# A decoder trunk on one core: five of the eleven block pairs of the last product by seven products of quarters

## The chip, the core and the metric

The kernel runs on one core of a Trainium2 chip. A core has a matrix engine (TensorE, PE in the profile, with its weight loads shown as PEld), a vector engine (VectorE, DVE), a scalar engine (ScalarE, ACT), a general engine (GpSimd, POOL) and a queue that issues most transfers (SyncE, SP). The metric is the device time of one launch in microseconds. Before the change it is 992.31 us, the median of three runs (992.31 to 992.92).

## The reference

The input is x, 256 tokens of 1024 features, in float32. Two layers follow each other, and each has the same three parts: a half-weighted SwiGLU feed-forward step, attention (dilated windows in the first layer, block-sparse in the second, whose keys and values are computed once from the stream after the first layer), and another half-weighted SwiGLU step. A final RMSNorm ends it. The change is in the last feed-forward step and what follows it:

```python
def swiglu(h, w_gate, w_up, w_down):
    return (jax.nn.silu(h @ w_gate) * (h @ w_up)) @ w_down

h = h + 0.5 * swiglu(rmsnorm(h, ffn2_norm[1]), ffn2_w_gate[1], ffn2_w_up[1], ffn2_w_down[1])
return rmsnorm(h, final_norm)
```

Here w_gate and w_up are 1024 x 2816 and w_down is 2816 x 1024. Everything is float32. The kernel reaches that by splitting each factor into a high part, rounded to a type that the matrix engine takes in one pass, and a low part, the remainder; a product is then three matmuls: high by high, high by low, low by high.

## The kernel before

The stream is kept with the features on the partitions (hT, eight tiles of 128 features by 256 tokens). A feed-forward step has two stages.

The gate and up stage is `ffn_blocks`. The 2816 hidden features are 22 blocks of 128, taken in eleven pairs. For a pair, the weights are loaded by SyncE into a raw tile (four of those exist), ScalarE writes their high parts (wh, line 153) and VectorE their low parts (wl, line 154); eight wh and eight wl buffers of 1024 columns exist. TensorE computes gate (f_g) and up (f_u) for a block (lines 193 and 196), and `close` makes the activation of the block: ScalarE and VectorE join the sums (lines 336, 337), VectorE scales (line 352), ScalarE applies the silu (line 353), GpSimd scales the up part (line 355), VectorE multiplies (line 356), and `parts_of` splits the product into a high part on ScalarE (line 94) and a low part on VectorE (line 90). The result is one act tile per block, high and low.

The last down product is `down_last`. Here the tokens are on the partitions of the output: two halves t of 128 tokens, and each output row has two halves c of 512 features. For each of the 22 blocks k, the act tile of k (128 x 128 for a token half) is the stationary factor and row block k of w_down the moving one. Two blocks come in one load of 1 MB (raw_f_d); each is split as above (wh_f_d, wl_f_d). Blocks 0 to 17 go to all accumulators in turn. The last four blocks are held back, so that the accumulators end one after another: for each, VectorE adds half of it to h (line 431), and `finish_part` and `finish` make the norm and send the rows out. The accumulator of the second token half and the second feature half is kept as two of 256 columns, so that the very last step is short. The order in which each engine takes its instructions comes from a scheduler that goes by the program's order, by what is ready in its own model, and by free buffers; on the chip each engine then runs its queue in that order and waits by semaphores.

The trace leaves digits out of names: dn_f21_d is dn_f_d there.

Of the kernel before, what the change touches and what calls it, by code (L numbers as in the profile page):

```python
# [25 lines left out]
NG = H // HG  # L26
ROT = 16
HALF = ROT // 2
LEAD = 4
EPS = 1e-6  # L30
SCALE = DH ** -0.5
# [31 lines left out]
def trunk(ctx: ExitStack, tc: tile.TileContext, a: dict, out: bass.AP):  # L63
    nc = tc.nc
    PS = bass.MemoryType.PSUM
    const = ctx.enter_context(tc.tile_pool(name="const", bufs=1))
    rawp = ctx.enter_context(tc.tile_pool(name="rawp", bufs=4))
    wp = ctx.enter_context(tc.tile_pool(name="wp", bufs=8))
    xp = ctx.enter_context(tc.tile_pool(name="xp", bufs=1))
# [30 lines left out]
    def trt(name):  # L100
        return trp.tile([P, 512], F32, tag="tr", name=name)
# [74 lines left out]
    def rows(w, k0, k, c0, n):  # L176
        return w[k0 * P:(k0 + k) * P, c0:c0 + n].rearrange("(k p) n -> p k n", p=P)

    def product(accs, xh, xl, ws, first, last):

        for ac, (wh, wl) in zip(accs, ws):
            nc.tensor.matmul(ac, xh, wh, start=first, stop=False)  # L182
        for ac, (wh, wl) in zip(accs, ws):
            nc.tensor.matmul(ac, xh, wl, start=False, stop=False)  # L184
        for ac, (wh, wl) in zip(accs, ws):
            nc.tensor.matmul(ac, xl, wh, start=False, stop=last)  # L186
# [94 lines left out]
    class Pieces:  # L281
# [6 lines left out]
        def load(self, u):  # L288
            while len(self.raws) <= min(u, len(self.specs) - 1):
                name, k, n, srcs = self.specs[len(self.raws)]  # L290
                raw = rawp.tile([P, k, n], F32, tag="raw", name=f"raw_{name}")
                for dst, src in srcs:
                    nc.sync.dma_start(raw if dst is None else raw[:, :, dst], src)
                self.raws.append(raw)

        def split(self, i):

            end = 2 * len(self.specs)
            while len(self.parts) <= min(i, end - 1):
# [37 lines left out]
        nc.vector.tensor_add(s, ac[:, :S], s)  # L337
        return s

    def ffn_blocks(name, wg, wu, norm, first=None, beside=()):  # L340

        blocks = []

        def both(f, pair):
            acs = [acc(f"{name}_{n}{f}") for n in "gu"]
            cols = slice(f % 2 * P, (f % 2 + 1) * P)
            products_t(acs, [[(wh[:, cols], wl[:, cols]) for wh, wl in w] for w in pair], norm.x, True, True)
            return acs

        def close(f, gate, up):  # L350
            g = joined(gate, f"{name}_g{f}")
            nc.vector.tensor_mul(g, g, norm.row)  # L352
            nc.scalar.activation(g, g, AF.Silu)  # L353
            u = joined(up, f"{name}_u{f}")
            nc.gpsimd.tensor_tensor(u, u, norm.row, op=ALU.mult)  # L355
            nc.vector.tensor_mul(g, g, u)  # L356
            x = atile([P, 2, S], F32R, name=f"act_{name}_{f}")
            parts_of(x[:, 0], x[:, 1], g)
            blocks.append(x)

        done = []

        def close_all():
            if done and norm.row is None:
                norm.spread()
            for args in done:
                close(*args)
            done.clear()

        for f in range(0, KF, 2):  # L370
            if f == 0 and first is not None:
                ws = opening(wg, wu, first)
            else:
                ws = zip(*[unit(f"{name}_{n}{f}", KD, S, [(None, rows(w, 0, KD, f * P, S))])
                           for n, w in (("g", wg), ("u", wu))])
            if f == 0:
                acs = [[(trt if i and n == "u" else acc)(f"{name}_{n}{i}") for n in "gu"] for i in range(2)]
                for k, pair in enumerate(ws):
                    for i in range(2):
                        for ac, (wh, wl) in zip(acs[i], pair):  # L380
# [24 lines left out]
        down_t(name, wd, blocks, after)  # L405


    def down_last(name, w, nk, blocks, h, weight, part, after, tail=4):


        segs = [[(0, 0, 512), (1, 0, 512)], [(0, 0, 512), (1, 0, 256), (1, 256, 256)]]
        accs = [[acc(f"dn_{name}_{t}_{c}_{o}")[:, :n] for c, o, n in segs[t]] for t in range(NT)]
        held = []

        def cols(t, ws):
            return [tuple(w[:, c * 512 + o:c * 512 + o + n] for w in ws) for c, o, n in segs[t]]

        for u in range(nk // 2):
            for i, ws in enumerate(unit(f"{name}_{u}", 2, D, [(None, rows(w, 2 * u, 2, 0, D))])):
                k = 2 * u + i  # L420
                if k < nk - tail:
                    for t in range(NT):
                        product(accs[t], *blocks[t][k], cols(t, ws), k == 0, False)
                else:
                    held.append((k, ws))
        for t in range(NT):
            for i, (c, o, n) in enumerate(segs[t]):
                for k, ws in held:
                    product(accs[t][i:i + 1], *blocks[t][k], cols(t, ws)[i:i + 1], False, k == nk - 1)
                hc = h[t][c][:, o:o + n]  # L430
                nc.vector.scalar_tensor_tensor(hc, accs[t][i], weight, hc, op0=ALU.mult, op1=ALU.add)
                part(t, slice(c * 512 + o, c * 512 + o + n))
            after(t)

    def out_t(name, pieces, base, blocks, norm, tail=3):
# [226 lines left out]
    w = a["a_w_qkv"][0]  # L662
# [12 lines left out]
        return [(n3, xkv, [wk]), (n5, xq, [wq]), (n3, xkv, [wv])]  # L675

    mixer("b", segs_b, a["b_w_o"][0], masks[:, 1, :], n6)
    blocks = ffn_blocks("f21", a["ffn2_w_gate"][1], a["ffn2_w_up"][1], n6)

    h = [[xp.tile([P, 512], F32, tag=f"kx{2 * t + c}", name=f"h_{t}_{c}") for c in range(2)] for t in range(NT)]  # L680
    for t in range(NT):
# [22 lines left out]
    def finish(t):  # L704
# [8 lines left out]
        for c in range(2):  # L713
            (nc.scalar, nc.sync)[c].dma_start(out[0, t * P:(t + 1) * P, c * 512:(c + 1) * 512], outs[t][c])

    down_last("f21_d", a["ffn2_w_down"][1], KF,
              [[tuple(x[:, i, t * P:(t + 1) * P] for i in range(2)) for x in blocks] for t in range(NT)],
              h, 0.5, finish_part, finish)


_INS = ["ffn1_w_gate", "ffn1_w_up", "ffn1_w_down", "ffn2_w_gate", "ffn2_w_up", "ffn2_w_down",
# [23 lines left out]
```

## Time and profile before

| what | value |
|---|---|
| median of three runs | 992.31 us |
| the profiled execution, its own time | 992.2 us |
| its span, first to last instruction | 990.4 us |
| granted TensorE clock, mean | 0.999 |
| TensorE busy | 979.6 us (99%) |
| VectorE busy | 731.3 us (74%) |
| ScalarE busy | 589.2 us (59%) |
| GpSimd busy | 163.6 us (17%) |
| the last down product, first to last matmul | 922.8 to 984.3 us |

A row of a timeline gives the start, the duration, the engine, the line, the operation, what is written and read, and in brackets the idle time ahead of it with what ended it. Matmuls overlap, so their durations are longer than the time from one start to the next; starts are what to compare. A row of a stage table gives the stretch, its length, then busy time and count of TensorE, its weight loads, VectorE, ScalarE and GpSimd, then the granted clock, the share of the transfer engines and their GB/s.

### The profile page before, as it was taken

The numbers are of one execution on the slowest core, as the hardware profiler recorded it, in microseconds if no ns is written. First come the engines' busy times: TensorE is split into PE (matmuls) and PEld (weight loads), VectorE is DVE, ScalarE is ACT, GpSimd is POOL, SyncE is SP. The second block draws the span as 40 slices with busy tenths as digits, with TensorE's granted clock in tenths as the row PEclk, the third lists the DMA queues.
The fourth block names the chain that finished last, engine by engine and source line by source line (L and its number), as shares of the span: only waits on it lengthen the run. The fifth ranks groups of instructions, "written<-read, shape, count | busy, mean of one in ns | idle before, by whom it ended". The sixth has DMA issues, their size and how long they took to land. (4 is left out here: it accounts for less than half of the span.)

```text
span 990.4 us, 15816 instructions
## 1 busy us (share of the span) xinstructions
PE 979.6 (99%) x5949; PEld 866.1 (87%) x5949; DVE 731.3 (74%) x1284; ACT 589.2 (59%) x1084; POOL 163.6 (17%) x195
## 2 busy tenths in 40 slices
PE   9999999999999999999999999999999999999997
PEld 6888888888899888888888888888889998888886
DVE  7988866667787887776678878666687778888542
ACT  6756554467776656645455666544676766655531
POOL 3211101122202211111021111111222032111000
PEclk9999999999999999999999999999999999999999
DMA  9876565654444466556646664666534445565511
GB/s 306 259 251 200 167 225 172 209 179 144 139 129 146 153 211 187 188 192 197 200 146 203 190 202 149 216 197 203 170 129 128 129 146 176 190 182 201 211 45 43
DMA packets 158398, 176.08 MB, mean 178 GB/s; under 512 B 3568, under 2 KB 152304, under 8 KB 158320
## 3 DMA queue, kind: packets, MB, share of 16 engines
q1 hardware_dynamic: 157888, 174.50, 54.8%
q8 instruction: 47, 0.77, 0.3%
q10 hardware_dynamic: 432, 0.55, 0.2%
q14 instruction: 31, 0.25, 0.1%
HBM read 173.99 MB, written 1.05 MB: 177 GB/s over the span
## 5 line engine op out<-in xcount | busy, mean ns | idle before, releaser
L193 PE MATMUL f_g<-x_n,wh_f_g 128*128 128x512 f32 x688 | 180.0, 394 | 0.0
L193 PE MATMUL f_u<-x_n,wh_f_u 128*128 128x512 f32 x688 | 177.6, 390 | 0.0
L193 PEld LDWEIGHTS f_u<-x_n,wh_f_u 128*128 128x128 f32 x688 | 129.0, 188 | 27.2
L193 PEld LDWEIGHTS f_g<-x_n,wh_f_g 128*128 128x128 f32 x688 | 124.1, 189 | 22.7
L355 POOL TENSOR_TENSOR j_f_u<-j_f_u,r_n 128x256 f32<-128x256 f32 x88 | 77.3, 880 | 378.1 <-DVE j_f_u L337 361.1
L193 PE MATMUL dn_f<-act_f,wh_f 128*128 128x512 f32 x528 | 126.5, 391 | 0.0
L154 DVE TENSOR_TENSOR wl_f_u<-raw_f_u,wh_f_u 128x1024 fp32r<-128x1024 f32 x86 | 120.8, 1406 | 1.8 <-ACT wh_f_u L153 1.7
L154 DVE TENSOR_TENSOR wl_f_g<-raw_f_g,wh_f_g 128x1024 fp32r<-128x1024 f32 x86 | 102.9, 1225 | 17.7 <-PE f_g L196 12.0
L193 PEld LDWEIGHTS dn_f<-act_f,wh_f 128*128 128x128 f32 x528 | 96.8, 188 | 18.6
L154 DVE TENSOR_TENSOR wl_f<-raw_f,wh_f 128x1024 fp32r<-128x1024 f32 x72 | 81.8, 1153 | 36.0 <-ACT wh_f L153 26.8
L196 PE MATMUL f_u<-x_n,wl_f_u 128*128 128x256 f32 x688 | 103.3, 283 | 0.0
L196 PE MATMUL f_g<-x_n,wl_f_g 128*128 128x256 f32 x688 | 102.7, 282 | 0.0
L196 PEld LDWEIGHTS f_g<-x_n,wl_f_g 128*128 128x128 f32 x688 | 96.4, 190 | 6.3
L153 ACT ACTIVATE wh_f_g<-raw_f_g 128x1024 fp32r<-128x1024 f32 x86 | 89.4, 1049 | 13.4 <-issue 6.0
L153 ACT ACTIVATE wh_f<-raw_f 128x1024 fp32r<-128x1024 f32 x72 | 67.3, 979 | 49.5 <-PE dn_f L193 30.3
L153 ACT ACTIVATE wh_f_u<-raw_f_u 128x1024 fp32r<-128x1024 f32 x86 | 86.6, 1047 | 15.7 <-PE f_g L193 10.9
L196 PEld LDWEIGHTS f_u<-x_n,wl_f_u 128*128 128x128 f32 x688 | 91.7, 192 | 0.1
L230 POOL TENSOR_TENSOR ss_n<-ss_n,sq_n 128x256 f32<-128x256 f32 x42 | 41.7, 992 | 246.5 <-ACT sq_n L229 245.6
L94 ACT ACTIVATE act_f<-j_f_g 128x256 fp32r<-128x256 f32 x88 | 36.5, 417 | 73.2 <-DVE j_f_g L356 73.1
L353 ACT ACTIVATE j_f_g<-j_f_g 128x256 f32<-128x256 f32 x88 | 36.7, 417 | 62.5 <-DVE j_f_g L352 62.1
L196 PEld LDWEIGHTS dn_f<-act_f,wl_f 128*128 128x128 f32 x528 | 68.1, 191 | 2.8
L196 PE MATMUL dn_f<-act_f,wl_f 128*128 128x256 f32 x528 | 69.0, 283 | 0.0
(213 smaller groups left out, 1798.1 us busy)
## 6 DMA issues: line engine op xcount, KB each, us to landing
raw_f_g<-in_ffn_w_gate_dram SPq DMA_DIRECT2D x43, 1024.0 KB, 5.4
raw_f_u<-in_ffn_w_up_dram SPq DMA_DIRECT2D x43, 1024.0 KB, 5.4
raw_f<-in_ffn_w_down_dram SPq DMA_DIRECT2D x24, 1024.0 KB, 5.0
raw_f_d<-in_ffn_w_down_dram SPq DMA_DIRECT2D x11, 1024.0 KB, 4.9
raw_f<-in_ffn_w_down_dram SPq DMA_DIRECT2D x12, 768.0 KB, 4.4
raw_qka<-in_a_w_qkv_dram SPq DMA_DIRECT2D x16, 512.0 KB, 4.6
raw_kvb<-in_kv_w_dram SPq DMA_DIRECT2D x12, 512.0 KB, 4.2
raw_va<-in_a_w_qkv_dram SPq DMA_DIRECT2D x4, 1024.0 KB, 5.0
```

The source lines that it names most:

```text
L94: nc.scalar.activation(hi, src, AF.Copy, scale=scale)
L153: nc.scalar.activation(wh, r, AF.Copy)
L154: nc.vector.tensor_sub(wl, r, wh.bitcast(F32))
L193: nc.tensor.matmul(ac, wh, flat(x), start=first and i == 0, stop=False)
L196: nc.tensor.matmul(ac[:, :S], wl, x[:, 0, :], start=False, stop=last and i == len(ws) - 1)
L230: nc.gpsimd.tensor_tensor(self.ss, self.ss, sq, op=ALU.add)
L353: nc.scalar.activation(g, g, AF.Silu)
L355: nc.gpsimd.tensor_tensor(u, u, norm.row, op=ALU.mult)
```

## The change

For five of the eleven pairs of blocks of the last product (2, 3, 5, 6 and 8, counted from 0) the product of a 2 x 2 arrangement of quarters (two token halves by two blocks, times two blocks by two feature halves) is formed by seven products instead of eight, with sums of quarters as factors. With A for the act quarters (token half, block) and B for the weight quarters (block, feature half), the left factors are A00, A01, A11 and four sums: A00 - A01, A11 - A01, A11 - A01 + A00, and A10 less the last. The right factors are B00, B10, B11 and four sums: B00 + B01, B11 + B01, the first of these plus B11, and that plus B10. Three of the seven go straight to one output quarter (c11, c12, c21); four go to accumulators of their own or are shared by several quarters (m1, m5, m6, m7). These are used by all five pairs and are collected once, after pair 8, into h.

- The sums of act are made in `ffn_blocks` by the new function `quarter_sums`, on VectorE, after the second block of a fast pair. Their high parts go to ScalarE at once, their low parts to VectorE one block later. The product of line 356 goes to a tile of its own for these pairs.
- The sums of the weights are made in `load`: one 1024-wide addition on VectorE and two 512-wide ones on GpSimd, into a tile from the four raw slots. A fast pair is then split into four wh and four wl tiles (1024, 512, 1024, 1024 columns) instead of two and two.
- Loads are written one pair ahead of the products. The accumulators are c11, c12, c21, m1, m5 in one pool and c22, m6, m7 in the other.
- The accumulator of the last quarter is one of 512 columns; only for the held blocks (pairs 9 and 10, as before four blocks) is it cut in two, and the second cut, "end", is a separate accumulator.
- The order of the matmuls changes everywhere in the product: three for one accumulator in a row, where the two accumulators of a token half alternated.

```diff
+FAST = (2, 3, 5, 6, 8)
...
+    def quarter_sums(x, hi, lo, name):
+        q = atile([P, 4, P], name=f"q_{name}")
+        x = x.rearrange("p a (t n) -> p (a t) n", n=P)
+        nc.vector.tensor_sub(q[:, :2], x[:, 0::3], x[:, 1:2].to_broadcast([P, 2, P]))
+        nc.vector.tensor_add(q[:, 2], q[:, 1], x[:, 0])
+        nc.vector.tensor_sub(q[:, 3], x[:, 2], q[:, 2])
+        rest = []
+        parts_of(hi, lo, flat(q), later=rest.append)
+        return rest
...
-            nc.vector.tensor_mul(g, g, u)
+            pair = f // 2
+            if sums is not None and pair in sums:
+                if f % 2 == 0:
+                    pairs[pair] = atile([P, 2, S], name=f"act2_{name}_{f}")
+                prod = pairs[pair][:, f % 2]
+            else:
+                prod = g
+            nc.vector.tensor_mul(prod, g, u)
             x = atile([P, 2, S], F32R, name=f"act_{name}_{f}")
-            parts_of(x[:, 0], x[:, 1], g)
+            parts_of(x[:, 0], x[:, 1], prod)
+            while rest:
+                rest.pop(0)()
+            if prod is not g and f % 2:
+                rest.extend(quarter_sums(pairs.pop(pair), *sums[pair], f"{name}_{f}"))
...
+    def down_last(name, w, blocks, sums, h, weight, part, after, tail=2):
+        c11, c12, c21, m1, m5 = [acc(f"dn_{name}_{n}") for n in ("11", "12", "21", "m1", "m5")]
+        c22, m6, m7 = [trt(f"dn_{name}_{n}") for n in ("22", "m6", "m7")]
...
+        def split(src, n):
+            wh, wl = [wp.tile([P, src.shape[1], 512], F32R, tag=tag, name=f"{tag}_{name}_{n}") for tag in ("wh", "wl")]
+            nc.scalar.activation(wh, src, AF.Copy)
+            nc.vector.tensor_sub(wl, src, wh.bitcast(F32))
+            return [(wh[:, i, :], wl[:, i, :]) for i in range(src.shape[1])]
+
+        def load(i):
+            raw = rawp.tile([P, 4, 512], F32, tag="raw", name=f"raw_{name}_{i}")
+            nc.sync.dma_start(raw.rearrange("p (k c) n -> p k (c n)", k=2), rows(w, 2 * i, 2, 0, D))
+            if i not in sums:
+                return split(raw[:, :2], f"{i}a") + split(raw[:, 2:], f"{i}b")
+            t = rawp.tile([P, 4, 512], F32, tag="raw", name=f"sum_{name}_{i}")
+            nc.vector.tensor_add(t[:, :2], raw[:, 0::3], raw[:, 1:2].to_broadcast([P, 2, 512]))
+            nc.gpsimd.tensor_tensor(t[:, 2], t[:, 0], raw[:, 3], op=ALU.add)
+            nc.gpsimd.tensor_tensor(t[:, 3], t[:, 2], raw[:, 2], op=ALU.add)
+            b11, b21 = split(raw[:, 0::2], f"{i}a")
+            b22, = split(raw[:, 3:], f"{i}b")
+            ta, tc = split(t[:, :2], f"{i}c")
+            tb, td = split(t[:, 2:], f"{i}d")
+            return b11, b21, b22, ta, tc, tb, td
+
+        def fast(i, ws):
+            b11, b21, b22, ta, tc, tb, td = ws
+            l7, l5, l6, l3 = [tuple(v[:, j * P:(j + 1) * P] for v in sums[i]) for j in range(4)]
+            x = [[blocks[t][2 * i + k] for k in range(2)] for t in range(NT)]
+            last = i == max(sums)
+            for n, ac, left, right in (("1", m1, x[0][0], b11), ("11", c11, x[0][1], b21), ("12", c12, l3, b22),
+                                       ("5", m5, l5, ta), ("7", m7, l7, tc), ("6", m6, l6, tb),
+                                       ("21", c21, x[1][1], td)):
+                add(n, ac, left, right, last and len(n) == 1)
+
+        def collect():
+            a, b, c, d = [atile([P, 512], name=f"co_{name}_{n}") for n in "abcd"]
+            nc.scalar.activation(a, m1, AF.Copy, scale=weight)
+            nc.vector.scalar_tensor_tensor(b, m6, weight, a, op0=ALU.mult, op1=ALU.subtract)
+            nc.gpsimd.tensor_tensor(h[0][0], h[0][0], a, op=ALU.add)
+            nc.vector.scalar_tensor_tensor(c, m7, weight, b, op0=ALU.mult, op1=ALU.subtract)
+            nc.vector.scalar_tensor_tensor(b, m5, -weight, b, op0=ALU.mult, op1=ALU.add)
+            nc.gpsimd.tensor_tensor(h[0][1], h[0][1], b, op=ALU.add)
+            nc.vector.scalar_tensor_tensor(d, m5, -weight, c, op0=ALU.mult, op1=ALU.subtract)
+            nc.vector.tensor_add(h[1][0], h[1][0], c)
+            nc.vector.tensor_add(h[1][1], h[1][1], d)
...
+        for i in range(pairs):
+            if i + 1 < pairs:
+                ahead.append(load(i + 1))
+            ws = ahead.pop(0)
+            if i in sums:
+                fast(i, ws)
+            elif i < pairs - tail:
+                for k in range(2):
+                    for t in range(NT):
+                        for c in range(2):
+                            add(*quarters[t][c], blocks[t][2 * i + k], ws[2 * k + c])
+            else:
+                held += [(2 * i + k, ws[2 * k:2 * k + 2]) for k in range(2)]
+        collect()
+        end = acc(f"dn_{name}_end")[:, :S]
...
+                cut = 512 if (t, c) != (1, 1) else S
+                for k, ws in held:
+                    add(n, ac[:, :cut], blocks[t][k], tuple(v[:, :cut] for v in ws[c]), k == KF - 1)
+                nc.vector.scalar_tensor_tensor(h[t][c], ac, weight, h[t][c], op0=ALU.mult, op1=ALU.add)
...
+                for k, ws in held:
+                    add("end", end, blocks[t][k], tuple(v[:, S:] for v in ws[1]), k == KF - 1)
```

More of the change, by code (lines that the diff above doesn't have):

```diff
@@ L338, in joined, with ffn_blocks @@
         return s
-    def ffn_blocks(name, wg, wu, norm, first=None, beside=()):
-        blocks = []
+    def quarter_sums(x, hi, lo, name):
[7 more added lines that the diff above has]
+        return rest
+    def ffn_blocks(name, wg, wu, norm, first=None, beside=(), sums=None):
+        blocks, pairs, rest = [], {}, []
         def both(f, pair):
@@ L405, in ffn, with add @@
         down_t(name, wd, blocks, after)
[L408 to L421, printed above, removed]
-                    for t in range(NT):
-                        product(accs[t], *blocks[t][k], cols(t, ws), k == 0, False)
-                else:
-                    held.append((k, ws))
+    def down_last(name, w, blocks, sums, h, weight, part, after, tail=2):
+        c11, c12, c21, m1, m5 = [acc(f"dn_{name}_{n}") for n in ("11", "12", "21", "m1", "m5")]
+        c22, m6, m7 = [trt(f"dn_{name}_{n}") for n in ("22", "m6", "m7")]
+        begun = set()
+        def add(n, ac, x, ws, last=False):
+            product([ac], *x, [ws], n not in begun, last)
+            begun.add(n)
+        def split(src, n):
[37 more added lines that the diff above has]
+            nc.vector.tensor_add(h[1][1], h[1][1], d)
+        quarters = [[("11", c11), ("12", c12)], [("21", c21), ("22", c22)]]
+        pairs = KF // 2
+        ahead, held = [load(0)], []
+        for i in range(pairs):
[6 more added lines that the diff above has]
+                for k in range(2):
+                    for t in range(NT):
+                        for c in range(2):
[4 more added lines that the diff above has]
+        end = acc(f"dn_{name}_end")[:, :S]
@@ L426, in down_last @@
         for t in range(NT):
-            for i, (c, o, n) in enumerate(segs[t]):
+            for c in range(2):
+                n, ac = quarters[t][c]
+                cut = 512 if (t, c) != (1, 1) else S
                 for k, ws in held:
[L429 to L432, printed above, removed]
+                    add(n, ac[:, :cut], blocks[t][k], tuple(v[:, :cut] for v in ws[c]), k == KF - 1)
+                nc.vector.scalar_tensor_tensor(h[t][c], ac, weight, h[t][c], op0=ALU.mult, op1=ALU.add)
+                part(t, slice(c * 512, c * 512 + cut))
@@ L433, in down_last @@
+            if t:
+                for k, ws in held:
+                    add("end", end, blocks[t][k], tuple(v[:, S:] for v in ws[1]), k == KF - 1)
+                hc = h[1][1][:, S:]
+                nc.vector.scalar_tensor_tensor(hc, end, weight, hc, op0=ALU.mult, op1=ALU.add)
+                part(t, slice(512 + S, 1024))
             after(t)
@@ L677, in trunk @@
     mixer("b", segs_b, a["b_w_o"][0], masks[:, 1, :], n6)
-    blocks = ffn_blocks("f21", a["ffn2_w_gate"][1], a["ffn2_w_up"][1], n6)
+    sums = {}
+    for n, i in enumerate(FAST):
+        if n < 4:
+            parts = ap_.tile([P, 2, 512], F32R, tag=("qkh", "qkl")[n % 2], name=f"left_{i}", bufs=2)
+            sums[i] = (parts[:, 0], parts[:, 1])
+        else:
+            sums[i] = tuple(xp.tile([P, 512], F32R, tag=f"kx{4 + 2 * (n - 4) + j}", name=f"left_{i}_{j}") for j in range(2))
+    blocks = ffn_blocks("f21", a["ffn2_w_gate"][1], a["ffn2_w_up"][1], n6, sums=sums)
     h = [[xp.tile([P, 512], F32, tag=f"kx{2 * t + c}", name=f"h_{t}_{c}") for c in range(2)] for t in range(NT)]
@@ L714, in finish @@
             (nc.scalar, nc.sync)[c].dma_start(out[0, t * P:(t + 1) * P, c * 512:(c + 1) * 512], outs[t][c])
-    down_last("f21_d", a["ffn2_w_down"][1], KF,
+    down_last("f21_d", a["ffn2_w_down"][1],
               [[tuple(x[:, i, t * P:(t + 1) * P] for i in range(2)) for x in blocks] for t in range(NT)],
-              h, 0.5, finish_part, finish)
+              sums, h, 0.5, finish_part, finish)
 _INS = ["ffn1_w_gate", "ffn1_w_up", "ffn1_w_down", "ffn2_w_gate", "ffn2_w_up", "ffn2_w_down",
```

## The prediction

> **What bounds the kernel now.** I read the page first: the busy line, the slices and the chain.
>
> ```profile
> span 990.4 us, 15816 instructions
> PE 979.6 (99%) x5949; PEld 866.1 (87%) x5949; DVE 731.3 (74%) x1284; ACT 589.2 (59%) x1084; POOL 163.6 (17%) x195
> ...
> PEclk9999999999999999999999999999999999999999
> ```
>
> TensorE is busy from end to end at full clock, so a matmul less is worth its start-to-start time. Busy time is pipelined and says nothing of that; the last product's timeline (PE only) and its tile view do.
>
> ```profile
> L182 PE MATMUL dn_f_d<-wh_f_d,act_f x110: 274/389/477, 922.8 to 983.7; 128*128 128x512 f32 x66, 128*128 128x256 f32 x44
> L153 ACT ACTIVATE wh_f_d<-raw_f_d x22: 1042/1060/1065, 905.6 to 962.1; 128x1024 fp32r<-128x1024 f32 x22
> L154 DVE TENSOR_TENSOR wl_f_d<-raw_f_d,wh_f_d x22: 1212/1224/1765, 908.7 to 963.2; 128x1024 fp32r<-128x1024 f32 x22
>   PE dn_f_d L186: 22.7, 14
> DMA to landing us min/median/max: 4.8/4.9/5.1
> ```
> ```profile
> 922.79 0.71 PE L182 MATMUL dn_f_d<-wh_f_d,act_f 128*128 128x512 f32 x2
> ...
> 964.68 0.64 PE L182 MATMUL dn_f_d<-wh_f_d,act_f 128*128 128x512 f32 x2
> ...
> 966.09 0.62 PE L182 MATMUL dn_f_d<-wh_f_d,act_f 128*128 128x512 f32 x3
> ...
> 973.06 0.40 PE L182 MATMUL dn_f_d<-wh_f_d,act_f 128*128 128x512 f32 x1
> ...
> 981.23 0.28 PE L182 MATMUL dn_f_d<-wh_f_d,act_f 128*128 128x256 f32 x1
> ...
> 983.98 0.28 PE L186 MATMUL dn_f_d<-wh_f_d,act_f 128*128 128x256 f32 x1
> ```
>
> Line 182 is one of three alike (182, 184, 186), so the product has 198 wide matmuls (512 columns) and 132 of 256. From 973.06 to 981.23 stand 36 wide ones, three to a product and all into one accumulator: 0.2267 us each. From 981.23 to 983.98 are 23 steps of 256: 0.1197 us. Before that two accumulators alternate: 964.68 to 966.09 is one token half of one block, six wide ones, 0.235 each; three blocks (964.68 to 973.06) take 8.38 us, 2.793 a block. Take 6 x 0.1197 off each: nine wide ones at 0.2305. The six alone give, with their neighbours (1.37 to 1.41), 0.232. So a wide matmul costs 0.2267 to 0.232 by its order. The stage runs from 922.79 to 984.10 (983.98 + 0.12): 61.31 us. The other rows say that the splits are ahead of it: ScalarE's splits wait 22.7 us, 14 times, for TensorE to free a buffer.
>
> **The change, part by part.**
>
> *Matmuls.* A fast pair has 7 products x 3 = 21 wide matmuls for 24. Steady: 4 plain pairs x 24 + 5 x 21 = 201. Held (pairs 9, 10): 36 wide, 24 of 256; before, the second half's second quarter was cut in two in every block, now only here. Every steady product is now three in a row into one bank, the order of the 973.06 run, but the bank changes after each three. Ends 0.2267 and 0.232; I take 0.229, between them and nearer the run whose order it has. Steady 201 x 0.229 = 46.0, held 36 x 0.2267 + 24 x 0.1197 = 11.0, start-up 0.1 (the first two matmuls lag): 57.15 us. Gain 61.31 - 57.15 = **4.2 us** (3.6 at 0.232, 4.7 at 0.2267). The 15 matmuls are 3.4 of it; the uncut quarter and the order the rest.
>
> In the Trainium skill, "TensorE: Matmul & The Clock Gate" (section Back-to-back issue gap) puts an isolated gap at N / 2.4 + 2.5 ns. By that 512 columns cost 0.2158 and 256 cost 0.1092, and the gain is 57.1 - 53.8 = 3.4 us; the rows here are 5 to 10% longer, so the trace decides.
>
> *Sums of act, in the stage before.* Per fast pair VectorE gets a subtraction over 256 columns, two steps over 128, and the low part of 512; ScalarE the high part of 512.
>
> ```profile
> 810.34 0.48 DVE L246 TENSOR_SCALAR diag_n<-ident,c_n 128x128 f32<-128x128 f32 x2 [0.83 <-POOL c_n L239]
> ...
> 897.56 2.36 DVE L154 TENSOR_TENSOR wl_f_g<-raw_f_g,wh_f_g 128x1024 fp32r<-128x1024 f32 x2 [0.91 <-PE f_g L196]
> ...
> 908.69 2.36 DVE L154 TENSOR_TENSOR wl_f_d<-raw_f_d,wh_f_d 128x1024 fp32r<-128x1024 f32 x2 [0.91 <-PE f_g L196]
> ```
> ```profile
> 832.00:843.10 11.10, 11.10 (x66) 9.80 (x65) 9.65 (x16) 6.56 (x13) 1.53 (x2) 1.00 0.73 227
> 898.80:909.90 11.10, 11.10 (x66) 9.81 (x65) 8.76 (x15) 6.74 (x13) 1.53 (x2) 1.00 0.58 189
> ```
> ```profile
> 913.59 1.11 PE L196 MATMUL f_g<-x_n,wl_f_g 128*128 128x256 f32 x8
> ```
>
> VectorE's share: 0.42 + 2 x 0.24 + 0.69 (a 128x512 row, quoted at the tail) = 1.6 us. A pair of gate and up lasts 11.1 us, and VectorE (the window rows' third busy figure) idles 11.10 - 9.65 = 1.45 at 832 and 2.3 from 898.8 on. The first fast pair may thus run VectorE 0.2 late, the others fit. What hides it is the lead: the last wl_f_g is written at 897.56 and its first low matmul is at 913.59, 16 us later. Cost nothing; without that cover, 5 x 1.6 = 8 us.
>
> *Sums of the weights and more splits, in the last product.* A fast pair takes on VectorE one 1024-wide addition, three 1024-wide low parts and one of 512: 4 x 1.18 (the 2.36 for two) + 0.69 = 5.4 us, for 2.4 before; on ScalarE at most 4 x 1.06 = 4.2, for 2.1; on GpSimd two additions of 512 columns. GpSimd has only 256-wide rows; twice 0.74, the fastest, gives 1.48 each, twice the slowest 1.93 gives 3.85.
>
> ```profile
> L355 POOL TENSOR_TENSOR j_f_u<-j_f_u,r_n x88: 735/787/1926, 25.8 to 923.0; 128x256 f32<-128x256 f32 x88
> ```
> ```profile
> 820.74 1.58 POOL L355 TENSOR_TENSOR j_f_u<-j_f_u,r_n 128x256 f32<-128x256 f32 x1 [3.14 <-DVE j_f_u L337]
> ```
> ```profile
> 889.70 1.76 DVE L154 TENSOR_TENSOR wl_f_u<-raw_f_u,wh_f_u 128x1024 fp32r<-128x1024 f32 x1
> 891.39 0.41 DVE L356 TENSOR_TENSOR j_f_g<-j_f_g,j_f_u 128x256 f32<-128x256 f32 x1
> 891.72 1.21 DVE L154 TENSOR_TENSOR wl_f_u<-raw_f_u,wh_f_u 128x1024 fp32r<-128x1024 f32 x1
> ```
>
> Beside a GpSimd step the same low part takes 1.76 for 1.21, so 0.55 is lost per 256 columns: 4 x 0.55 = 2.2 a pair, and VectorE needs **7.6 us** per fast pair against TensorE's 21 x 0.229 = 4.8. That is over; the plain pairs (2.4 against 5.5) and the lead must pay. Starts of the pairs on TensorE: 922.8, 928.3, 933.8 (pair 2), 938.6, 943.4, 948.9 (5), 953.7, 958.5, 964.0 (8), 968.8 (held).
>
> ```profile
> 925.12 1.21 DVE L154 TENSOR_TENSOR wl_f_d<-raw_f_d,wh_f_d 128x1024 fp32r<-128x1024 f32 x1
> ```
>
> This is VectorE's eighth low part, the end of pairs 0 to 3, at 926.3. With the same eight buffers it will then have done pairs 0 to 2: pair 2 at 7.6 in place of pairs 2 and 3 at 4 x 1.18, so about 929.2. From there 3, 4, 5, 6, 7, 8 take 4 x 7.6 + 2 x 2.4 and end at 964.4; the last factor of pair 8 is wanted at 964.0 + 18 x 0.229 = 968.1. Cover 3.7 us; the tipping price is 8.5 us a pair. Cost nothing.
>
> The Trainium skill ("SBUF — State Buffer", section Who interferes with whom) says that a VectorE instruction with two SBUF inputs and a GpSimd one that reads SBUF exclude each other for the whole instruction. The 1.58 and 1.76 rows agree in kind. By it the pair costs 5.4 + 2 x 1.48 = 8.4 us, just inside the cover, and the sum stays.
>
> *Buffers and loads.* A sum takes one of the four raw slots, so a load waits for the pair two before. A load lands in 4.9 us; by this schedule the load of pair 6 can start when pair 3's sums are done, near 937, and VectorE wants it near 947. Hidden; if each fast pair had to wait, 4.9 us each. Per pair four of eight wh slots are used, so a fast pair's splits wait for the second pair before it, as they do for TensorE now.
>
> *The collection and the tail.* One ScalarE copy, six VectorE steps and two GpSimd additions of 512 columns.
>
> ```profile
> 975.99 0.69 DVE L431 SCALAR_TENSOR_TENSOR h<-dn_f_d,h 128x512 f32<-128x512 f32 x1 [11.56 <-PE dn_f_d L186]
> 976.71 0.69 DVE L702 TENSOR_TENSOR out<-h,gfin 128x512 f32<-128x512 f32 x1
> ...
> 982.98 0.42 DVE L431 SCALAR_TENSOR_TENSOR h<-dn_f_d,h 128x256 f32<-128x256 f32 x1
> ...
> 984.29 0.42 DVE L431 SCALAR_TENSOR_TENSOR h<-dn_f_d,h 128x256 f32<-128x256 f32 x1 [0.44 <-PE dn_f_d L186]
> ```
>
> 6 x 0.69 = 4.1 us from the end of pair 8, beside 11.0 us of held matmuls. The first half's sums may come 1 to 2 us late; the second half's final ones, 8 us on, not. The addition at 982.98 becomes 512 wide (+0.27) and eats into 0.44 idle. Nothing; uncovered, at most 4 us. TensorE isn't held up: "end" takes a bank of m1 or m5, read by then.
>
> Sum: 992.2 (the profiled execution, 0.1 under the median) - 4.2 = 988.0; against the median 992.31, **988.1**.
>
> **The rivals.**
>
> *A: as summed*, 988.1, 987.3 to 989.0 by the matmul's price. For it: the 22.7 us of waiting for TensorE. Against: VectorE's 7.6 over 4.8.
>
> *B: the sums come partly late.* VectorE's pair costs about 9.3: 4 x (9.3 - 8.5) = 3.2 lost of 4.2, 991.3. For it: the first fast pairs fall where VectorE has 1.45 us left; against: nothing measured reaches 9.3.
>
> *C: slower.* The chain of one fast pair runs in a row: addition, two GpSimd steps, split, low part, with VectorE's queue waiting behind it. At the slowest GpSimd row 1.18 + 2 x 3.85 + 1.06 + 1.18 = 11.1 us; 4 x (11.1 - 8.5) = 10.4 late, 998.5. It decides from 8.5 + 4.2 / 4 = 9.6 on, so from 3.1 us per GpSimd step. For it: the 1.58 row gives 3.16; against: at 1.48 the chain is 6.4, and another pair's steps can fill it.
>
> **How the numbers follow.** A 0.74, B 0.11, C 0.15. This measurement can't tell under 0.2% (2.0 us) from no change: faster means below 990.3. A and a third of B lie there: 0.78; the rest of B 0.07 within; C 0.15. The time is A's. The range takes A with both matmul prices and some slack, and B: 986.9 to 991.5; C is left out, under 0.2.
>
> **What would show it.** Right: 201 + 36 wide matmuls in the last product, 57 us, no gaps on TensorE; ScalarE's splits still waiting for TensorE; wl_f_g as early as before. Wrong: TensorE idle ahead of a seventh product from VectorE's low part of the last sums, GpSimd steps over 3.1 us, loads issued late, or gate and up longer than 11.1 us a pair. A steady product longer than 0.70 would make the gain smaller without any wait.

## The result, and the profile after

The changed kernel takes 995.57 us (median of 6 runs, 995.21 to 996.11) against 992.32 for the kernel before beside it: ratio 1.0032, 95% interval 1.0022 to 1.0042. It is slower by about 3.2 us; the forecast was 988.1, faster by 4.2. In the experiments below, one execution of the filled kernel (2499 us) and one of the kernel with the additions on VectorE (1608 us) were slow ones and are left out of the ratios and groups.

The page of the changed kernel, its span, TensorE's busy line and the granted clock in 40 slices (the columns are as in the page before):

```profile
span 994.3 us, 15758 instructions
PE 977.4 (98%) x5880; PEld 862.5 (87%) x5880; DVE 760.7 (77%) x1325; ACT 598.2 (60%) x1100; POOL 191.7 (19%) x207
...
PEclk9999999999999999999999999999999999999899
```

There are 69 matmuls fewer, and TensorE is busy 2.2 us less while the span is 3.9 us longer: about 6 us of idle time are new. The slice of the clock that now shows an 8 is where the last product begins. The list of TensorE's waits names the place (engine, what it wanted, who ended the wait; total, times, longest):

```profile
PE h L782 <- ACT h L783: 5.8, 1, 5.8
```

The row is new, and it is the only one from 900 us on; the other rows, 1.4 us each at most, lie earlier. Line 782 (685 before) is the sixteen transposes of h that stand between the gate and up products and the last product, four to a tile; line 783 is ScalarE's copy of a transposed tile into h. The transposes use the three banks of the pool "tr", so the fourth tile waits for ScalarE's first copy. TensorE's timeline of the kernel before at that place (start, duration):

```profile
920.11 1.12 PE L196 MATMUL f_u<-x_n,wl_f_u 128*128 128x256 f32 x8
921.07 1.97 PE L685 MATMUL h<-ident,hT 128*128 128x128 f32 x16
922.79 0.71 PE L182 MATMUL dn_f_d<-wh_f_d,act_f 128*128 128x512 f32 x2
```

and of the changed kernel:

```profile
920.23 1.12 PE L197 MATMUL f_u<-x_n,wl_f_u 128*128 128x256 f32 x8
921.19 1.47 PE L782 MATMUL h<-ident,hT 128*128 128x128 f32 x12
928.48 1.12 PE L782 MATMUL h<-ident,hT 128*128 128x128 f32 x4 [5.82 <-ACT h L783]
929.24 0.78 PE L183 MATMUL dn_f_d<-wh_f_d_0a,act_f 128*128 128x512 f32 x1
929.82 0.63 PE L185 MATMUL dn_f_d<-wl_f_d_0a,act_f 128*128 128x512 f32 x1
...
933.66 0.42 PE L185 MATMUL dn_f_d<-wl_f_d_0a,act_f 128*128 128x512 f32 x1
933.91 0.39 PE L187 MATMUL dn_f_d<-wh_f_d_0a,act_f 128*128 128x512 f32 x1
```

Two things are to be seen. The last product begins at 929.24 instead of 922.79, and its first matmuls stand 0.427 us apart (929.82 to 933.66 is nine steps) instead of 0.227. The stage table of the changed kernel (stretch, length, busy time and count of TensorE, weight loads, VectorE, ScalarE, GpSimd; clock; transfers) shows the clock beside them:

```profile
921.10:928.50 7.40, 1.58 (x16) 1.34 (x14) 6.21 (x8) 5.30 (x10) 4.18 (x3) 0.89 0.00 0
928.50:934.00 5.50, 5.50 (x16) 4.49 (x17) 3.92 (x7) 2.21 (x5) 1.64 (x1) 0.53 0.67 200
934.00:983.00 49.00, 49.00 (x218) 40.59 (x217) 40.22 (x36) 24.28 (x27) 14.04 (x8) 1.00 0.36 128
```

The granted clock over the 5.5 us that begin with the end of the wait is 0.53. Then it is 1.00 again, and TensorE is never idle inside the product.

The account of the 3.9 us between the two profiled spans: gate and up end 0.1 later; the transposes take 929.24 - 921.19 = 8.05 us instead of 1.72, so 6.3 more; the slow matmuls cost 2.2 (eleven steps from 929.24 to 933.91, about 0.2 each); the product without that is 988.01 - 929.24 - 2.2 = 56.6 us instead of 61.3, so 4.7 less; the tail behind the last matmul is 6.3 in both. 0.1 + 6.3 + 2.2 - 4.7 = 3.9.

Why ScalarE's first copy of h comes late stands in ScalarE's timeline of the changed kernel:

```profile
921.54 0.42 ACT L368 ACTIVATE j_f_g<-j_f_g 128x256 f32<-128x256 f32 x1 [1.30 <-DVE j_f_g L367]
921.86 1.04 ACT L449 ACTIVATE wh_f_d_2a<-raw_f_d 128x1024 fp32r<-128x1024 f32 x1
922.81 0.61 ACT L449 ACTIVATE wh_f_d_2b<-raw_f_d 128x512 fp32r<-128x512 f32 x1
925.09 0.42 ACT L95 ACTIVATE act_f<-j_f_g 128x256 fp32r<-128x256 f32 x1 [1.66 <-DVE j_f_g L378]
925.41 1.04 ACT L449 ACTIVATE wh_f_d_2c<-sum_f_d 128x1024 fp32r<-128x1024 f32 x1
926.36 1.04 ACT L449 ACTIVATE wh_f_d_2d<-sum_f_d 128x1024 fp32r<-128x1024 f32 x1
927.30 0.36 ACT L337 ACTIVATE j_f_g<-f_g 128x256 f32<-128x256 f32 x1
927.57 0.37 ACT L337 ACTIVATE j_f_u<-f_u 128x256 f32<-128x256 f32 x1
927.83 1.08 ACT L783 ACTIVATE h<-h 128x512 f32<-128x512 f32 x2
```

The same queue of the kernel before has its last joins at 921.21 and the copies at 921.74:

```profile
921.21 0.36 ACT L336 ACTIVATE j_f_g<-f_g 128x256 f32<-128x256 f32 x1
...
921.74 2.05 ACT L686 ACTIVATE h<-h 128x512 f32<-128x512 f32 x4
```

So the copies stand in order behind the closing steps of block 20 (which wait for VectorE and GpSimd) and behind four splits of pair 2, a fast pair. The delay builds up: the first join of the gate product of blocks 18, 19, 20 and 21 starts 1.9, 3.0, 4.8 and 6.1 us later than before. VectorE's queue shows what delays block 20's close further:

```profile
921.75 1.22 DVE L459 TENSOR_TENSOR sum_f_d<-raw_f_d 128x1024 f32<-128x1024 f32 x1
923.59 1.47 DVE L378 TENSOR_TENSOR j_f_g<-j_f_g,j_f_u 128x256 f32<-128x256 f32 x1 [0.61 <-POOL j_f_u L370]
```

In the kernel before the same multiplication was:

```profile
917.58 0.42 DVE L356 TENSOR_TENSOR j_f_g<-j_f_g,j_f_u 128x256 f32<-128x256 f32 x1 [0.92 <-POOL j_f_u L355]
```

The sum of pair 3's weights stands ahead of block 20's multiplication. Beside that sum GpSimd's scaling of block 20 takes 1.64 us (0.74 before), and the multiplication then takes 1.47 us beside GpSimd's addition (`L460`, 923.51 to 924.77) where it took 0.42 before.

### The profile page after: what moved, and what is told of

It reads as the page before. It is cut to its first block, busy times and chain, and to the rows that moved or that the text cites. A ratio compares the mean times of both kernels' runs of the same rounds, so it can differ in the third digit from the quotient of the medians.

```text
span 994.3 us, 15758 instructions
## 1 busy us (share of the span) xinstructions
PE 977.4 (98%) x5880; PEld 862.5 (87%) x5880; DVE 760.7 (77%) x1325; ACT 598.2 (60%) x1100; POOL 191.7 (19%) x207
## 5 line engine op out<-in xcount | busy, mean ns | idle before, releaser
L370 POOL TENSOR_TENSOR j_f_u<-j_f_u,r_n 128x256 f32<-128x256 f32 x88 | 86.1, 980 | 371.3 <-DVE j_f_u L338 349.0
L155 DVE TENSOR_TENSOR wl_f_u<-raw_f_u,wh_f_u 128x1024 fp32r<-128x1024 f32 x86 | 118.3, 1376 | 1.8 <-ACT wh_f_u L154 1.7
L95 ACT ACTIVATE act_f<-j_f_g 128x256 fp32r<-128x256 f32 x78 | 32.3, 417 | 67.5 <-DVE j_f_g L378 67.4
```

The lines of the kernel that those rows point to most:

```text
L155: nc.vector.tensor_sub(wl, r, wh.bitcast(F32))
```

## The experiments

Theory Q says that the loss is the queue at the end of the gate and up products: late close, then ScalarE, then the copies of h, then TensorE and its clock. Theory V says that VectorE has too much to do, wherever the copies stand. All kernels below are the changed kernel with one edit, unless said otherwise.

**Copies of h early.** The transposes and copies move into the gate and up products, one tile per pair of blocks, where h's source is long complete:

```diff
-    for t in range(NT):
-        for c in range(2):
-            tr = trt(f"h_{t}_{c}")
...
+    def turn_h(t, c):
+        tr = trt(f"h_{t}_{c}")
...
+    turns_h = [lambda: None] * 4 + [lambda t=t, c=c: turn_h(t, c) for t in range(NT) for c in range(2)]
-    blocks = ffn_blocks("f21", a["ffn2_w_gate"][1], a["ffn2_w_up"][1], n6, sums=sums)
+    blocks = ffn_blocks("f21", a["ffn2_w_gate"][1], a["ffn2_w_up"][1], n6, beside=turns_h, sums=sums)
```

> The changed kernel with one thing moved: the sixteen transposes that turn the stream for the last norm, and ScalarE's four copies of them, are made in the middle of gate and up, one tile per pair from pair 5 to pair 8, and no longer between gate and up and the last product. Theory Q (queue): TensorE's 5.8 us hole is the fourth transpose waiting for ScalarE's copies, which stand in ScalarE's queue behind the splits of pair 2. Then the hole (6.3 us) and the ten slow matmuls behind it (2.2 us) go, the product keeps its 56.6 us, and the time is 995.6 - 8.5 = 987.1, between 986.8 and 988.2. Theory V (VectorE): VectorE is late by its own load of sums of act, and whatever TensorE needs next will be late too. Then a hole of several us moves to the start of the product and the time stays over 990.

Measured: 993.4 us (ratio 1.0012, 1.0003 to 1.0021). The wait of 5.8 us and the slow matmuls are gone; the product starts right behind the gate and up products, at 922.88, and ends at 983.07. But that is 60.2 us, not 56.6: TensorE now waits inside it. Its timeline and then the other engines' queues in this run:

```profile
942.55 0.50 PE L185 MATMUL dn_f_d_m<-wl_f_d_3d,left 128*128 128x512 f32 x1 [0.22 <-DVE wl_f_d_3d L450]
...
944.78 0.50 PE L185 MATMUL dn_f_d<-wl_f_d_4a,act_f 128*128 128x512 f32 x1 [0.57 <-DVE wl_f_d_4a L450]
...
974.15 0.50 PE L185 MATMUL dn_f_d<-wl_f_d_10b,act_f 128*128 128x512 f32 x1 [1.26 <-DVE wl_f_d_10b L450]
```
```profile
937.90 1.23 DVE L459 TENSOR_TENSOR sum_f_d<-raw_f_d 128x1024 f32<-128x1024 f32 x1 [2.90 <-DMA raw_f_d<-in_ffn_w_down_dram]
...
940.17 2.32 DVE L450 TENSOR_TENSOR wl_f_d_3d<-sum_f_d,wh_f_d_3d 128x1024 fp32r<-128x1024 f32 x1
942.42 2.31 DVE L450 TENSOR_TENSOR wl_f_d_4a<-raw_f_d,wh_f_d_4a 128x1024 fp32r<-128x1024 f32 x1
...
952.66 1.21 DVE L450 TENSOR_TENSOR wl_f_d_6c<-sum_f_d,wh_f_d_6c 128x1024 fp32r<-128x1024 f32 x1
957.50 1.23 DVE L450 TENSOR_TENSOR wl_f_d_6d<-sum_f_d,wh_f_d_6d 128x1024 fp32r<-128x1024 f32 x1 [3.62 <-ACT wh_f_d_6d L449]
```
```profile
951.14 3.88 POOL L460 TENSOR_TENSOR sum_f_d<-sum_f_d,raw_f_d 128x512 f32<-128x512 f32 x1 [7.50 <-DVE sum_f_d L459]
955.10 1.28 POOL L461 TENSOR_TENSOR sum_f_d<-sum_f_d,raw_f_d 128x512 f32<-128x512 f32 x1
```

VectorE's queue stood still for 2.90 us behind a load and for 3.62 us behind pair 6's chain (addition on VectorE, two on GpSimd, split on ScalarE, low part on VectorE): GpSimd's first addition took 3.88 us, the second 1.28, and only then came ScalarE's split (956.41). The waits listed are 2.1 us and, with the steps beside them, the product is 3.6 us over 56.6. VectorE also reaches the collection late (974.02, with 9 us of the product left; 968.05, with 11 left, in the last experiment) and the tail is 8.3 us instead of 6.3. Against the kernel before: -1.1 in the product, +2.0 in the tail, +0.1: +1.0, as measured. Q is right about the place of the loss, but its time, 987.1, missed by 6 us; V's time, over 990, held, though the new waits stand inside the product and not at its start. In the changed kernel the first wait starts the product 6.4 us later than here (929.24 against 922.88). VectorE has that much more time, which explains why that kernel shows no wait inside the product.

**The control:** the same move in the kernel before.

> The kernel before with the same move and nothing else, as the control. In its trace the transposes take 1.72 us without a hole; moved, they take the same time elsewhere. Theories Q and V both: 992.3, within 0.4. If the move is worth something by itself (over 0.5 us), that much of the gain of the run beside it isn't the hole's.

Measured: 992.25 us (ratio 1.0000, 0.9991 to 1.0009). The move is worth nothing by itself, so what it brings in the other kernels is the lateness taken away.

**The slow matmuls alone.** Twenty-four matmuls whose result is not used stand ahead of the fourth transposed tile, so that TensorE waits without being idle:

```diff
+            if t and c:
+                keep = acc("keep")
+                for i in range(24):
+                    nc.tensor.matmul(keep, fill[:, :P], fill, start=True, stop=True)
             tr = trt(f"h_{t}_{c}")
```

> The changed kernel with 24 matmuls that nothing uses put on TensorE between the third and the fourth tile of transposes, about 5.2 us, into the hole. If the ten matmuls of 0.43 us behind the hole are the clock that fell in it, they go back to 0.227 and the time falls by 2.2 us, to 993.4 (993.0 to 993.8); the hole itself stays, filled. If they are slow for another cause (late factors, the copies), the time stays at 995.6.

Measured: 993.63 us (ratio 1.0014, 1.0005 to 1.0023), 1.9 us under the changed kernel. The matmuls behind the wait stand 0.23 apart from the second on:

```profile
922.35 5.34 PE L783 MATMUL keep<-fill 128*128 128x512 bf16 x24
928.35 0.66 PE L786 MATMUL h<-ident,hT 128*128 128x128 f32 x4 [0.65 <-ACT h L787]
928.76 0.48 PE L183 MATMUL dn_f_d<-wh_f_d_0a,act_f 128*128 128x512 f32 x1
929.08 0.40 PE L185 MATMUL dn_f_d<-wl_f_d_0a,act_f 128*128 128x512 f32 x1
...
929.54 0.40 PE L183 MATMUL dn_f_d<-wh_f_d_0a,act_f 128*128 128x512 f32 x1
```

About 2 us of the loss are the clock that the idle time costs, apart from the idle time itself, as forecast (993.0 to 993.8).

**Only the sums of act.** They are made as in the change, but the last product uses plain products throughout: no sums of weights, no collection.

```diff
-              sums, h, 0.5, finish_part, finish)
+              {}, h, 0.5, finish_part, finish)
...
-        collect()
+        if sums:
+            collect()
```

> The changed kernel with the sums of act made as there, but not used: all eleven pairs of the last product go by eight products, so there are no sums of weights, no wider splits and no collection. The order of the matmuls and the uncut quarter stay. Theory Q: the sums of act are covered, TensorE has no hole over 0.5 us, and the product takes 216 x 0.2267 + 11.0 = 60.0 for 61.3: 991.0 (990.5 to 991.5). Theory V: VectorE is late from the sums of act alone, the hole is still 3 us or more, and the time is over 993.5.

Measured: 995.24 us (ratio 1.0030, 1.0019 to 1.0041), not 991.0. V's time (over 993.5) held. ScalarE's joins of block 21 are late here too, behind the splits of pairs 2 and 3:

```profile
920.98 1.04 ACT L449 ACTIVATE wh_f_d_2b<-raw_f_d 128x1024 fp32r<-128x1024 f32 x1
...
923.82 0.36 ACT L337 ACTIVATE j_f_g<-f_g 128x256 f32<-128x256 f32 x1
```

TensorE waits 2.50 us ahead of the fourth tile and then has seven slow matmuls. I had put the whole wait down to pair 2's sums of weights; that was too narrow. The splits ahead of the joins are not the cause by themselves: the kernel of the next experiment, which has no sums, has the same splits in the same order there, and its TensorE doesn't wait. Its rows:

```profile
918.94 1.04 ACT L449 ACTIVATE wh_f_d_2b<-raw_f_d 128x1024 fp32r<-128x1024 f32 x1
...
921.79 0.36 ACT L337 ACTIVATE j_f_g<-f_g 128x256 f32<-128x256 f32 x1
```

All of this part of the queue stands 2.0 us later with the sums of act, and 2.7 later when set against TensorE, which itself runs 0.6 earlier in the run with the sums. The lateness is older than that: the join of block 10 is already 1.7 us late by the same measure (860.81 against 859.71), and that of block 19, after the last sums, 1.8. It stays although VectorE is busy for only 8.46 of the 11.10 us from 910.00 to 921.10. So it isn't a lack of VectorE's time there. The sums also change the order in which the scheduler sets VectorE's and ScalarE's steps; whether their time or that order keeps the queue late, no run here separates.

**The new order alone.** No pair by seven products, no sums at all (the `collect` line guarded as above):

```diff
-FAST = (2, 3, 5, 6, 8)
+FAST = ()
```

> No pair by seven products: the new order of the plain products, the uncut lower right quarter and the whole-pair loads stay, no sums of act, no sums of weights, no collection. Theory S (the lateness at the end of the gate and up products is made by the sums): the transposes of h start and end as in the kernel before, the product takes about 60.1 us against 61.3, and the time is 991.1 us. Rival O (the new order of loads and splits puts weight splits ahead of the last joins on ScalarE by itself): the fourth transpose still waits 1 to 2.5 us and the time is 992.5 to 994.5 us.

Measured: 991.06 us (ratio 0.9988, 0.9979 to 0.9996), as theory S forecast (991.1), and no wait ahead of the product. The order of loads and splits does no harm, and with the uncut quarter and the new order of matmuls it is worth 1.2 us. The difference to the run before it, 4.2 us, is what the sums of act cost by themselves, with the order of steps that comes with them.

**Without pair 2.**

```diff
-FAST = (2, 3, 5, 6, 8)
+FAST = (3, 5, 6, 8)
```

> Pairs 3, 5, 6 and 8 by seven products, pair 2 plainly; the copies of h stay where the change has them. Theory S2 (sums of act make 2.5 us of the wait ahead of the fourth transpose, the weights' sums of pair 2 the rest): the wait falls to about 2.5 us, the slow matmuls to about 1.4 us, and with a product of 57.3 us the time is about 992.3 us. Rival S3 (the next fast pair's weight sums come up in its place): the wait stays near 5.8 us and the time is 995.5 to 996.5 us.

Measured: 992.71 us (ratio 1.0001, 0.9992 to 1.0010). The wait is 2.95 us, nearer S2's 2.5 than S3's 5.8. The edit takes away pair 2's sums of act as well as those of its weights, and pair 3's chain of additions still stands ahead of block 20's close, so the 2.95 us can't be put down to the sums of act alone. What the sums of act alone make is the 2.50 us above; all the rest of the change makes the other 3.3. The executions fall into two groups, 991.3 to 991.8 and 992.7 to 993.4; the profiled one is of the first and keeps the full clock behind the wait:

```profile
926.00:927.00 1.00, 1.00 (x7) 0.82 (x6) 1.00 (x4) 1.00 (x3) 0.59 (x1) 1.00 0.06 4
```

The next run has two groups too, 991.2 and 992.4 to 993.1; its profiled execution is of the second, with the clock at 0.50 for 3.4 us, and its mean clocks differ by group (0.998 against 0.996 to 0.997). The 1.2 to 1.4 us between the groups are what the slow matmuls cost in the run with the sums of act alone, so there the second group is probably that in which the clock drops. Without pair 2 the mean clocks don't tell the groups apart (0.998 in all executions but one, 0.996), so what makes them stays open.

**Additions on VectorE only.** GpSimd's two additions per pair go to VectorE; the copies of h stay where the change has them.

```diff
-            nc.gpsimd.tensor_tensor(t[:, 2], t[:, 0], raw[:, 3], op=ALU.add)
-            nc.gpsimd.tensor_tensor(t[:, 3], t[:, 2], raw[:, 2], op=ALU.add)
+            nc.vector.tensor_add(t[:, 2], t[:, 0], raw[:, 3])
+            nc.vector.tensor_add(t[:, 3], t[:, 2], raw[:, 2])
```

> The changed kernel with one edit: the two additions per pair that GpSimd did stand on VectorE; the copies of h stay where the change has them. Theory G (the slow additions on GpSimd and what they do to VectorE beside them make the part of the wait that the sums of act don't make): the wait ahead of the fourth transpose falls from 5.8 to 2.5 to 3.0 us, and the time is 992.3 + 0.1 - 4.7 + 2.5 to 3.0, with up to 1.4 us of slow matmuls behind it: 990.2 to 992.1 us. Rival W (the splits and sums of pair 2 stand ahead of the last joins, whoever adds): VectorE has 1.2 us more to do per pair there, the wait stays at 5.8 us or grows and the time is 995.5 to 997.5 us.

Measured: 992.72 us (ratio 1.0001, 0.9992 to 1.0011). The wait is 3.45 us, a little over theory G's 2.5 to 3.0 and far from W's 5.8, though VectorE does more; the time is 0.6 us over G's upper bound. Having the additions on GpSimd, and not the splits of pair 2 by themselves, makes 2.4 of the 3.3 us by which the wait is longer than with the sums of act alone.

**Three fast pairs, copies of h early.** The move of h as above, and

```diff
-FAST = (2, 3, 5, 6, 8)
+FAST = (3, 5, 7)
```

> The copies of h inside the gate and up products as in the first experiment, and three pairs (3, 5 and 7) by seven products in place of five. Theory V (without the hole the product is held by VectorE where fast pairs stand next to each other, and the tail by a collection that VectorE reaches late): with a plain pair between, the waits inside the product go, the tail is 6.3 us again, the product takes 60.1 - 3 x 0.68 = 58.1 us and the time is 989.2 us. Rival L (each fast pair waits for its own load and GpSimd chain, wherever it stands): about 0.7 us of wait per fast pair remains and part of the late tail, 991 to 992.5 us.

Measured: 989.01 us (ratio 0.9967, 0.9955 to 0.9980). No wait of TensorE in or ahead of the product, and a tail of 6.3 us. Theory V's 989.2 held, and rival L's wait per fast pair did not appear. The edit changes two things, how many fast pairs there are and how they stand; this run doesn't say which of them lets VectorE keep up.

**Five fast pairs, copies of h early, additions on VectorE.** The two edits together:

> The first experiment (copies of h early, five fast pairs) with the two additions per pair that GpSimd did put on VectorE. Theory C (VectorE and GpSimd delay each other: low parts of 2.3 us beside additions of up to 3.9 us): VectorE gains more than the 1.2 us per pair that it takes on, the waits in the product shrink from 3.6 us to about 1 and the time is 990 to 991.5 us. Rival T (VectorE's total work binds): it has some 6 us more to do in the product, the waits grow and the time is 995 to 998 us.

Measured: 987.62 us (ratio 0.9953, 0.9941 to 0.9966), the fastest of all, and below the 990 to 991.5 of theory C; rival T's 995 is ruled out. Against the changed kernel the move of h alone gave 2.2 us, the additions on VectorE alone 2.9, and both together 8.0. TensorE has no wait from 915 us on, and works at full clock (stage table):

```profile
934.00:983.00 49.00, 45.65 (x213) 38.11 (x211) 42.10 (x49) 25.00 (x34) 5.08 (x7) 1.00 0.35 125
```

The product runs from 922.87 to 979.49, 56.6 us. VectorE's queue around pair 6, which stood still for 3.62 us above, is now without a gap:

```profile
946.33 1.22 DVE L459 TENSOR_TENSOR sum_f_d<-raw_f_d 128x1024 f32<-128x1024 f32 x1
...
948.60 0.68 DVE L460 TENSOR_TENSOR sum_f_d<-sum_f_d,raw_f_d 128x512 f32<-128x512 f32 x1
...
951.70 1.23 DVE L450 TENSOR_TENSOR wl_f_d_6d<-sum_f_d,wh_f_d_6d 128x1024 fp32r<-128x1024 f32 x1
952.84 1.22 DVE L450 TENSOR_TENSOR wl_f_d_7a<-raw_f_d,wh_f_d_7a 128x1024 fp32r<-128x1024 f32 x1
```

A fast pair costs VectorE 952.84 - 946.33 = 6.5 us including the two additions that it took on. Pair 8 takes 6.5 as well (955.11 to 961.62). In the first experiment pair 8 took 7.5 without them (960.92 to 968.38), and pair 6, with its wait, 8.9 (949.79 to 958.65). The wait of about 2.9 us for pair 5's load is in both. So VectorE's total work was not the limit; being held up by GpSimd was.

## Why the prediction was wrong

**Matmuls: right, a little low.** Forecast 57.15 us and a gain of 4.2; without the slow stretch the changed kernel takes 56.6, and so does the last experiment, a gain of 4.7. A wide matmul of the new order costs 0.2267 where nothing slows it, the lower end that I gave; the change of bank after each three costs nothing. (At that price my own sum gives a gain of 4.6, not the 4.7 that I wrote beside it.)

**Sums of act: this step failed.** "What hides it is the lead", the 16 us by which wl_f_g is ready, is true for TensorE's low matmuls of gate and up, which end 0.1 us later than before. But the same VectorE queue also closes each block, and behind the last close stand ScalarE's copies of h, for which TensorE waits with no lead at all. I never looked at the sixteen transposes between the two products. "Cost nothing" measured 4.2 us (only the sums of act against the new order alone): a product that starts 2.7 us later, and 1.4 of slow matmuls. The 8 us that I wrote for the case "without that cover" asked about the wrong cover, and were no price for this wait.

**Sums of the weights: the same hole, and GpSimd's price.** VectorE ended the last factor of pair 8 at 969.80, 5.4 us after the 964.4 of my sum. That is more than the cover of 3.7; TensorE didn't wait only because the product was 6.45 late. The sums of the first fast pairs are made at the end of the stage before, where the step did not look: they make the other 3.3 us of the wait. Without the wait (copies early) the cover fails. VectorE ends pair 2 at 932.9 instead of 929.2, which spends all of it, and pair 6 takes 8.9 us, over my tipping point of 8.5, though pair 8, without a standstill, takes 7.5: the sum of busy times left out that VectorE's queue stands still behind a chain. That is rival C's mechanism, addition, two GpSimd steps, split, low part; it decided there not at 3.1 us per GpSimd step throughout, but with one step of 3.88. In the kernel as changed TensorE doesn't wait for that chain inside the product, so C's time of 998.5 and its place were wrong; but GpSimd's additions are part of the wait ahead of the product, which is 5.82 us with them and 3.45 without. From "SBUF — State Buffer" of the Trainium skill the prediction took the rule that the two engines exclude each other, and said the pair would cost 8.4 us by it. The rows agree with the rule: 3.88 is 1.28 plus the 2.7 us of VectorE's steps up to 953.8. The cost came as longer steps (2.31 for 1.22) and as waiting.

**Buffers and loads: mostly right.** Loads land in 4.8 us. VectorE does wait 2.9 us for the load of pair 5 when the copies are early. That load takes the slot of pair 2's sums, which VectorE last reads until 932.9, and it has landed by 937.9; I had worked the case out for pair 6 alone. The fastest kernel has the same wait, and there it costs nothing.

**Collection and tail: right for the kernel as changed** (6.3 us in both). With VectorE late it is not: 8.3 in the first experiment.

**What would show it:** I named TensorE idle ahead of a seventh product, long GpSimd steps, late loads, longer gate and up. In the changed kernel TensorE didn't wait for a seventh product, gate and up ended 0.1 us later in all, and GpSimd's additions of 512 columns take 1.26 to 2.16 us, under the 3.1 that I named. The idle time stood ahead of the product's first matmul, which I had not named, and it cost the clock as well, which no step of mine priced.

## What to carry to other kernels

Work put on an engine "with lead" has to be followed through every queue that it stands in up to the end of the stage: the last thing of a stage that TensorE waits for may have no lead even where the bulk has 16 us. Here it paid, before relieving TensorE by work on other engines, to move the small steps at the seam between two products out of those engines' queues, and to keep the additions of a chain on VectorE rather than split them between VectorE and GpSimd. A wait can hide a second one behind it, so after a hole is closed the whole stage has to be read again.

## What the runs showed of the hardware

- A wait of TensorE cost up to 2.2 us here beyond its own length. The granted clock falls to 0.50 for stretches of one length: with one-microsecond rows of the stage table, 925.3 to 928.7 in the runs with the sums of act alone and with the additions on VectorE (3.4 us), 926.9 to 933.7 in the changed kernel (6.8, twice that). The rows of the run with the sums of act alone:

```profile
925.00:926.00 1.00, 1.00 (x5) 1.00 (x6) 1.00 (x2) 0.99 (x3) 0.78 (x1) 0.64 0.37 94
926.00:927.00 1.00, 1.00 (x4) 0.71 (x4) 1.00 (x2) 0.83 (x2) 0.00 (x0) 0.50 1.03 426
...
928.00:929.00 1.00, 1.00 (x5) 0.77 (x4) 0.83 (x2) 0.00 (x0) 0.00 (x0) 0.66 0.17 66
```

The Trainium skill, "TensorE: Matmul & The Clock Gate" (Part 1), has a free-running window of about 3.4 us behind the half clock, which agrees with these lengths; executions with and without a drop, as it would allow, could be the two groups of times. It also has a whole idle window as the condition, and here a wait of 2.50 us was enough in one run, while one of 2.95 was not in another. But TensorE only transposes on both sides of these waits: in the run with 2.50, no other matmul runs from 921.2 to 925.5, which is 4.3 us. If the transposes don't count as work, which no run here tests, each drop seen fits the condition, and a longer wait without a drop fits too if the window lay otherwise. What decides stays open.

- An addition of 128x512 takes GpSimd 1.28 us alone and up to 3.88 beside VectorE, and VectorE 0.68; a 128x1024 low part of VectorE takes 1.22 alone and 2.31 beside GpSimd's addition. The low part is held up for about one addition of GpSimd's; the addition of 3.88 us (951.14 to 955.02) is held up while three of VectorE's steps run one after another (950.93 to 953.87).
